# Token pieces of 384, 384, 320 and a regrouped merge in a hybrid encoder layer

## Chip, cores and metric

One core of one Trainium2 chip runs one launch of the kernel. The metric is the device time of a launch in microseconds.

## The reference

One layer of a streaming encoder for T = 1088 tokens (1024 of a new stream, 64 of a continued one) at a width of 1024, in fp32. P = RMSNorm(x) @ w_in gives the inputs of four branches of width 512, their gate paths and four merge gates of 1024 columns each. Cut to what the change touches:

```python
u = jnp.stack([u_a, u_b, u_c, u_d], axis=2)          # four branches, (B, T, 4, 512)
y_br = jnp.einsum('btnc,ncd->btnd', u, p['w_down'])  # each (512 -> 1024)
gates = jax.nn.sigmoid(merge.reshape(bsz, t, N_BRANCH, D_MODEL))
mixed = jnp.sum(gates * y_br, axis=2)
out = rms_norm(mixed @ p['w_out'], p['norm_post'])   # y = x + out
```

A is a gated linear recurrence, B a chunked state-space scan (SSD), C a convolution with a LayerNorm, D stick-breaking attention.

## The kernel before

**Operands.** Activations lie transposed: channels on the 128 partitions, tokens along the free axis. Each fp32 operand is split into a high and a low fp32r part (ScalarE copies, VectorE subtracts), and a product is three matmuls, high by high, high by low, low by high (`mm3`, L104 to L107). `hh` and `hl` hold the normed input, `w_hi` and `w_lo` 128 output columns of a weight.

**Pieces.** The tokens are cut into three pieces, `SPL` = 256, 384, 448, and `hh`, `hl` are three tiles each, one per piece. `project` (L172) makes one piece of one 128-column chunk of P: 8 steps of the contraction by 3 matmuls, 24. `proj` (L176) loads a chunk's weights and does the three pieces. The pieces are also the steps in which matrix work is fed between the steps of other chains (`Feed`, L142): `feed.step(n)` issues n pieces. In the head, pieces 0, 1, 2 of two v chunks follow the transposes of the token tiles that they need (L340 to L346).

**Order.** PE runs in the order written in the program (L188). The other engines' instructions are ordered ahead of time by a planner, from costs of its own and priorities, and run in that order; `high_priority` raises an instruction by some number of places (`W_PRIO` = 300 for weight splits). All DMAs are issued by SP, in one queue.

**Stages**, by the profile: head to 57 us, projections and attention to 585, the recurrence to 742, LayerNorm to 895 and the SSD scan to 1238, both with the merge fed in between, then the gates of the last branch to 1335, its down projection to 1383, the output to the end.

**Merge** (L674). For each of three branches, `merge` walks over eight blocks d of 128 output columns. In a step it makes a gate piece (24 matmuls, a sigmoid on ScalarE), then the down piece of the same tokens (`down`, L668: 12 matmuls), and VectorE multiplies the two out of PSUM and adds them to `mt[d]` (L696, or L698 and L699). PSUM has three buffers `pj` for both kinds. Gate weights and down weights come from the same two buffers `w_hi`, `w_lo`; one load of 512 KB holds the down weights of two blocks.

**Last branch** (L947 to L983). All its gates are made first, into `sga`. Then for each d come three down pieces, evacuated by VectorE (L967, L968), copied and split into `mh` and `ml` (L969, L974), while the output weights are split into `wo` and `wp` (L982, L983). `mh` and the first half of the output weights lie in the buffers of `hh` and `hl`. The down weights are loaded for two blocks at a time, into the other of the two buffers (L971).

**SSD scan** (L810). Each of nine chunks of 128 tokens loads `xb` (two buffers), and has four parts with feed steps of 2, 1 and 2 between them; L871 and L878 belong to `second`, L838 and L845 to `first` of the next chunk, and L881 is the last reader of `xb`.

Of the kernel before, what the change touches and what calls it, by code (L numbers as in the profile page):

```python
# [18 lines left out]
SPL = ((0, 256), (256, 384), (640, 448))  # L19
NM = 448  # L20
WHERE = [(j, i * 128 - t0) for i in range(9) for j, (t0, n) in enumerate(SPL) if t0 <= i * 128 < t0 + n]
# [5 lines left out]
LNA, LNB = (2, 2, 2), 5  # L27
# [18 lines left out]
def encoder_step(ctx, tc, x, prm, win, wdt, wdn, wout, lwa, lwx, ckT, cv_, ssd0, npre, npost, dtb, alog, dskip,  # L46
# [62 lines left out]
    def rstd(st, r, n, w=1):  # L109
        """Second quarter of st = (first quarter / n + eps) ** -0.5, with one Newton step after the table's root."""  # L110
        a, y, v, t = (st[:r, j * w:j * w + w] for j in range(4))
        V.tensor_scalar(v, a, 1.0 / n, EPS, op0=OP.mult, op1=OP.add)
        S.activation(t, v, AF.Sqrt)
        V.reciprocal(y, t)
        V.tensor_tensor(t, y, y, op=OP.mult)
        V.tensor_tensor(t, t, v, op=OP.mult)
        V.tensor_scalar(t, t, -0.5, 1.5, op0=OP.mult, op1=OP.add)
        V.tensor_tensor(y, y, t, op=OP.mult)

    class Work:  # L120
        """A chain of matrix work: its first stretch fetches operands, each later one is a piece of the tokens."""
# [20 lines left out]
    class Feed:  # L142
        """Matrix work issued between the steps of another chain."""
# [28 lines left out]
    def project(p, n, i, hi, lo):  # L172
        for k in range(8):
            mm3(p[:, :n], hi[:, k, :], lo[:, k, :], hh[i][:, k, :], hl[i][:, k, :], k == 0, k == 7)

    def proj(chunk, evac, pt=pj, done=None):  # L176
        hi, lo = weights(win[chunk])
        yield
        for i, (t0, n) in enumerate(SPL):
# [12 lines left out]
    def head(hd, g_bc, tiles):  # L192
        w = len(tiles)
        st = hd.tile([128, 4 * w], FT, name="st", bufs=4)
        xs = []
        for e, i in enumerate(tiles):
            r = 128 if i < 8 else 64
            xt = hd.tile([128, D], FT, name="xt", bufs=9)
            dma(xt[:r], x[i * 128:i * 128 + r, :])
            if i == 0:  # L200
                dma(g_bc, ap(npre, 0, [[0, 128], [1, D]]))
            if r < 128:
                V.memset(st[r:, e:e + 1], 1.0)
            sq = hd.tile([128, D], FT, name="sq", bufs=1)
            S.activation(sq[:r], xt[:r], AF.Square, accum_out=st[:r, e:e + 1])
            xs.append(xt)
        rstd(st, 128, D, w)
        for e, i in enumerate(tiles):
            r = 128 if i < 8 else 64
            hn = hd.tile([128, D], FT, name="hn", bufs=4)  # L210
            V.scalar_tensor_tensor(hn[:r], xs[e][:r], st[:r, w + e:w + e + 1], g_bc[:r], op0=OP.mult, op1=OP.mult)
            j, o = WHERE[i]
            nk = 8 if i % 2 else 4
            for q in range(0, 8, nk):
                p = pz() if nk == 8 else pg()
# [63 lines left out]
    # convolution module  # L279
# [29 lines left out]
    def spill(chunk, dst):  # L309
        def evac(t0, n, p):  # L310
            g = cp.tile([128, NM], FT, name="t3", bufs=3)
# [6 lines left out]
    def v_chunk(c, lag=2):  # L318
        def evac(t0, n, p):
            vT = cp.tile([128, NM], FT, name="t3", bufs=3)  # L320
            S.activation(vT[:, :n], p[:, :n], AF.Copy)
            dma(vT_o[c][:, t0:t0 + n], vT[:, :n])

            def turn():
                pt = pg()
                j0, nb = t0 // 128, n // 128
                for j in range(0, n, 128):
                    r = min(128, n - j)
                    PE.transpose(pt[:r, j:j + 128], vT[:, j:j + r], ident)
                S.activation(v_tok[:, j0:j0 + nb, c * 128:(c + 1) * 128],  # L330
                             pt[:, :nb * 128].rearrange("p (j c) -> p j c", c=128), AF.Copy)
                if n % 128:
                    S.activation(v_tok[:64, 8, c * 128:(c + 1) * 128], pt[:64, nb * 128:nb * 128 + 128], AF.Copy)
            feed.defer(lag, turn)
        yield from proj(C_V + c, evac)

    s0 = Work(both(v_chunk(0, 1), v_chunk(1, 1)))
# [31 lines left out]
    def k_chunk(c):  # L369
        def evac(t0, n, p):  # L370
            kt = cp.tile([128, NM], FT, name="t3", bufs=3)
# [178 lines left out]
    # RG-LRU, inputs of the SSD  # L550
# [99 lines left out]
    # merge of the branches  # L650
    ut = ctx.enter_context(tc.tile_pool(name="ut", bufs=1, reuse_waits="tile"))
    tp_ = ctx.enter_context(tc.tile_pool(name="tp", bufs=3, reuse_waits="tile"))
    mp = ctx.enter_context(tc.tile_pool(name="mp", bufs=1, reuse_waits="tile"))
    mt = [mp.tile([128, T], FT, name=f"m{d}") for d in range(8)]
# [13 lines left out]
    def down(wh, wl, e, us, i, n):  # L668
        p = pj()
        for k in range(4):  # L670
            mm3(p[:, :n], wh[:, 4 * e + k, :], wl[:, 4 * e + k, :], us[i][0][:, k, :], us[i][1][:, k, :], k == 0, k == 3)
        return p

    def merge(bi):  # L674
# [3 lines left out]
        nwd = weights(wdn[b, 0])  # L678
        yield
        for d in range(8):  # L680
            hi, lo = nxt
            if d % 2 == 0:
                wh, wl = nwd

            def gate(i, n):
                p = pj()
                project(p, n, i, hi, lo)
                sg = tp_.tile([128, NM], FT, name="sg")
                S.activation(sg[:, :n], p[:, :n], AF.Sigmoid)  # L689
                return sg  # L690

            def mix(i, t0, n, sg):
                p = down(wh, wl, d % 2, us, i, n)
                m = mt[d][:, t0:t0 + n]
# [5 lines left out]
            sgs = [gate(i, n) for i, (_, n) in enumerate(SPL)] if d + bi == 0 else None  # L700
            for i, (t0, n) in enumerate(SPL):
                mix(i, t0, n, sgs[i] if sgs else gate(i, n))
                if i == 0 and d < 7:
                    nxt = weights(win[C_MG + 8 * b + d + 1])
                    if d % 2:
                        nwd = weights(wdn[b, (d + 1) // 2])
# [4 lines left out]
    # LayerNorm of the convolution module  # L711
# [3 lines left out]
    with tc.tile_pool(name="ln", bufs=1, side="right", reuse_waits="tile") as ln:  # L715
# [16 lines left out]
        for i, (t0, n) in enumerate(SPL):  # L732
            p = pg()
            for k in range(8):
                for q, hx in enumerate((hh, hl)):
                    PE.matmul(p[:16, :n], wd2[:, k, :], hx[i][:, k, :], start=k == 0 and q == 0, stop=k == 7 and q == 1)  # L736
            S.activation(dtr[:, t0:t0 + n], p[:16, :n], AF.Copy)
        feed.step()
# [14 lines left out]
        for i, (t0, n) in enumerate(SPL):  # L753
# [13 lines left out]
            feed.step(2)  # L767
# [15 lines left out]
            feed.step(2)  # L783
# [18 lines left out]
    # SSD scan  # L802
# [7 lines left out]
    class Chunk:  # L810
# [3 lines left out]
        def first(self):  # L814
# [6 lines left out]
            xb = self.xb = sp_.tile([128, 8, 128], FT, name="xb")  # L821
# [107 lines left out]
    for i in range(9):  # L929
# [4 lines left out]
        feed.step(2)  # L934
        if prev:
            prev.fourth()
        feed.step()
        ch.second()
        feed.step(2)
        prev = ch  # L940
    prev.third()
    feed.step()
# [5 lines left out]
    us = [load_u(b, i) for i in range(3)]  # L948
    sgp = ctx.enter_context(tc.tile_pool(name="sgp", bufs=1, side="right", reuse_waits="tile"))
# [4 lines left out]
    mh = [hp.tile([128, 8, n], FR, name=f"mh{i}", tag=f"hh{i}") for i, (_, n) in enumerate(SPL)]  # L954
    wo = [[], []]
    for i, (_, n) in enumerate(SPL):
        wt_ = hp.tile([128, n // 128, 1024], FR, name=f"wo{i}", tag=f"hl{i}")
        wo[0] += [wt_[:, k, :] for k in range(n // 128)]
    ml = []
    nwd = weights(wdn[b, 0])  # L960
    for d in range(8):
        if d % 2 == 0:
            wh, wl = nwd
        g = sga[d]
        for i, (t0, n) in enumerate(SPL):
            p = down(wh, wl, d % 2, us, i, n)
            V.tensor_tensor(g[:, t0:t0 + n], p[:, :n], g[:, t0:t0 + n], op=OP.mult)  # L967
            V.tensor_tensor(g[:, t0:t0 + n], mt[d][:, t0:t0 + n], g[:, t0:t0 + n], op=OP.add)  # L968
            S.activation(mh[i][:, d, :], g[:, t0:t0 + n], AF.Copy)  # L969
        if d in (0, 2, 4):  # L970
            nwd = weights(wdn[b, d // 2 + 1])  # L971
        l_ = mp.tile([128, T], FR, name=f"ml{d}", tag=f"m{d}")
        for i, (t0, n) in enumerate(SPL):
            V.tensor_sub(l_[:, t0:t0 + n], g[:, t0:t0 + n], mh[i][:, d, :].bitcast(FT))  # L974
# [11 lines left out]
    for i in range(9):  # L986
        r = 128 if i < 8 else 64
        j, o = WHERE[i]
        xr = ut.tile([128, D], FT, name="xr", tag=f"uh{i % 2}")
        dma(xr[:r], x[i * 128:i * 128 + r, :])  # L990
        st = tp_.tile([128, 4], FT, name="ost", bufs=2)
        sq = ut.tile([128, 512], FT, name="osq", tag="uh2")
        yo = ut.tile([128, D], FT, name="yo", tag=f"ul{i % 2}")
        for e in range(2):
            p = pj() if e == 0 else pg()
            for k in range(8):
                w = wo[e][k]
                mm3(p[:r], mh[j][:, k, o:o + r], ml[k][:, i * 128:i * 128 + r], w[:, 0:512], w[:, 512:1024],
# [73 lines left out]
```

## Time and profile before

| | us |
|---|---|
| median of 3 runs | 1493.87 |
| lowest, highest | 1492.25, 1494.49 |
| profiled execution, span from first to last instruction | 1490.9 |
| PE busy | 1460.1 |
| VectorE busy | 921.1 |
| ScalarE busy | 588.5 |

The page gives the profiled execution's span; its time as a launch is not listed beside it, so the median stands for it, 3.0 us above the span. PE is the matmul engine, PEld its weight loads, DVE is VectorE, ACT ScalarE, SP the engine that issues DMAs. L106 is line 106 of the kernel before.

### The profile page before, as it was taken

How to read it: one execution, taken by the hardware profiler on the slowest of the kernel's cores; microseconds unless marked ns; L12 is line 12 of the kernel's file. 1: busy time of each engine (PE TensorE's matmuls, PEld its weight loads, DVE VectorE, ACT ScalarE, POOL GpSimd, SP SyncE). 2: the span in 40 equal slices, each digit the busy share in tenths (PEclk: the TensorE clock that was granted, in tenths of full speed). 3: DMA queues.
4: the chain of work that ended last, by engine and by line, in shares of the span. 5: the costliest groups of instructions: out<-in, count | busy, mean ns of one | idle time of the engine just before them, and what ended most of it. 6: DMA issues, size and time to landing. Idle time of an engine off the chain costs nothing.

```text
span 1490.9 us, 23008 instructions
## 1 busy us (share of the span) xinstructions
PE 1460.1 (98%) x9157; PEld 1360.5 (91%) x9157; DVE 921.1 (62%) x1379; ACT 588.5 (39%) x1000; POOL 118.9 (8%) x157
## 2 busy tenths in 40 slices
PE   6999999999999999999999999999999999999997
PEld 5898999999999998999999999999999999999885
DVE  6289589579769955677765554656655541019433
ACT  6323434443453344666644322333332332124211
POOL 0003212231221222000000000000000000000000
PEclk9999999999999999999999999999999999999999
DMA  6232212313212323454433354222621234113322
GB/s 209 75 87 63 72 61 68 103 44 89 92 46 87 98 87 109 138 117 107 116 124 116 110 169 142 82 68 83 196 78 57 75 88 148 51 43 113 99 85 71
DMA packets 103339, 144.17 MB, mean 97 GB/s; under 512 B 20800, under 2 KB 82112, under 8 KB 103232
## 3 DMA queue, kind: packets, MB, share of 16 engines
q1 hardware_dynamic: 103232, 142.71, 31.9%
q8 instruction: 72, 1.18, 0.3%
q14 instruction: 35, 0.29, 0.1%
HBM read 97.95 MB, written 40.53 MB: 93 GB/s over the span
## 4 chain that ended last, share of the span: by engine, by line
PE 87%; issue 6%; DVE 4%; DMA 1%; ACT 1%; POOL 1%; SPq 0%; DVEq 0%; POOLq 0%; ACTq 0%
PE pj L105 24%; PE pj L106 24%; PE pj L107 24%; PE pg L468 2%; PE pg L450 2%; PE pg L106 1%; PE pg L107 1%; PE pg L105 1%; DVE cvo L239 1%; PE pz L417 1%; PE pz L418 1%; PE pg L878 1%; PE pg L736 1%; PE pg L871 1%; DMA g_bc<-in_npre_dram 0%
## 5 line engine op out<-in xcount | busy, mean ns | idle before, releaser
L105 PE MATMUL pj<-hh,w_hi 128*128 128x384 f32 (+2 forms) x1920 | 637.6, 332 | 1.7 <-ACT hh L220 1.7
L106 PE MATMUL pj<-hl,w_hi 128*128 128x384 f32 (+2 forms) x1920 | 631.8, 329 | 1.8 <-DVE hl L221 1.8
L107 PE MATMUL pj<-hh,w_lo 128*128 128x384 f32 (+2 forms) x1920 | 631.5, 329 | 0.0
L105 PEld LDWEIGHTS pj<-hh,w_hi 128*128 128x128 f32 x1920 | 363.6, 189 | 16.6 <-issue 2.1
L106 PEld LDWEIGHTS pj<-hl,w_hi 128*128 128x128 f32 x1920 | 363.7, 189 | 14.4 <-DVE hl L221 2.6
L107 PEld LDWEIGHTS pj<-hh,w_lo 128*128 128x128 f32 x1920 | 363.5, 189 | 11.0
L98 DVE TENSOR_TENSOR w_lo<-w_raw,w_hi 128x1024 fp32r<-128x1024 f32 x96 | 117.5, 1224 | 226.9 <-ACT w_hi L97 226.7
L97 ACT ACTIVATE w_hi<-w_raw 128x1024 fp32r<-128x1024 f32 x96 | 101.7, 1060 | 281.7 <-PE pj L106 262.6
L239 DVE SCALAR_TENSOR_TENSOR cvo<-cbuf,p_t,cvo 128x1118 f32<-128x1118 f32 x120 | 165.6, 1380 | 2.1
L105 PE MATMUL pj<-uh,w_hi 128*128 128x384 f32 (+2 forms) x384 | 126.2, 329 | 0.0
L107 PE MATMUL pj<-uh,w_lo 128*128 128x384 f32 (+2 forms) x384 | 126.2, 329 | 0.0
L106 PE MATMUL pj<-ul,w_hi 128*128 128x384 f32 (+2 forms) x384 | 126.1, 328 | 0.0
L438 DVE TENSOR_TENSOR_SCAN fb<-fb,ones 128x128 f32<-128x128 f32 (+8 forms) x68 | 90.0, 1324 | 38.0 <-POOL fb L435 37.4
L435 POOL TENSOR_SCALAR_AFFINE_SELECT beta<-beta 128x128 f32<-128x128 f32 (+1 forms) x72 | 78.2, 1086 | 14.4 <-ACT beta L431 13.7
L698 DVE TENSOR_TENSOR sg<-pj,sg 128x256 f32<-128x256 f32 (+2 forms) x48 | 25.7, 535 | 84.9 <-PE pj L107 80.6
L689 ACT ACTIVATE sg<-pj 128x256 f32<-128x256 f32 (+2 forms) x72 | 33.7, 468 | 112.2 <-PE pj L107 112.0
L105 PEld LDWEIGHTS pj<-uh,w_hi 128*128 128x128 f32 x384 | 72.7, 189 | 2.3
L106 PEld LDWEIGHTS pj<-ul,w_hi 128*128 128x128 f32 x384 | 72.6, 189 | 2.2
L107 PEld LDWEIGHTS pj<-uh,w_lo 128*128 128x128 f32 x384 | 72.6, 189 | 2.2
L435 POOL TENSOR_SCALAR_AFFINE_SELECT fb<-fb 128x128 f32<-128x128 f32 (+1 forms) x72 | 38.2, 530 | 449.2 <-ACT fb L430 354.4
L439 DVE TENSOR_TENSOR beta<-beta,fb 128x128 f32<-128x128 f32 (+8 forms) x68 | 50.3, 740 | 4.3 <-POOL beta L435 0.7
L452 ACT ACTIVATE wT<-pg 128x512 f32<-128x512 f32 (+3 forms) x96 | 43.3, 485 | 18.1 <-PE pg L450 17.8
(313 smaller groups left out, 1683.0 us busy)
## 6 DMA issues: line engine op xcount, KB each, us to landing
w_raw<-in_win_dram SPq DMA_DIRECT2D x80, 512.0 KB, 3.7
w_raw<-in_wdn_dram SPq DMA_DIRECT2D x16, 512.0 KB, 3.6
xt<-in_x_dram SPq DMA_DIRECT2D x8, 512.0 KB, 10.5
xbc<-xs SPq DMA_DIRECT2D x8, 512.0 KB, 2.6
xb<-xbc SPq DMA_DIRECT2D x8, 512.0 KB, 4.9
w_raw<-in_wout_dram SPq DMA_DIRECT2D x8, 512.0 KB, 3.7
xr<-in_x_dram SPq DMA_DIRECT2D x8, 512.0 KB, 3.8
out_y_dram<-yo SPq DMA_DIRECT2D x16, 256.0 KB, 2.3
```

The costliest lines, as they stand in the source:

```text
L97: S.activation(hi, r3, AF.Copy)
L98: V.tensor_sub(lo, r3, hi.bitcast(FT))
L105: PE.matmul(out, ah, bh, start=first, stop=False)
L106: PE.matmul(out, ah, bl, start=False, stop=False)
L107: PE.matmul(out, al, bh, start=False, stop=last)
L239: V.scalar_tensor_tensor(out[:, :n], b[:, i:i + n], w[:, i:i + 1], out[:, :n], op0=OP.mult, op1=OP.add)
L435: G.affine_select(t_[s, 1024 - w:1024], t_[s, 1024 - w:1024], pattern=[[-1, w]], compare_op=OP.is_gt, fill=fill, base=0, channel_multiplier=1)
L438: V.tensor_tensor_scan(F[:, rev], F[:, rev], ones[:, 0:1].to_broadcast([128, n]), 1.0, OP.mult, OP.mult)
L439: V.tensor_tensor(B[:, L:1024], B[:, L:1024], F[:, L + 1:1025], op=OP.mult)
L450: PE.transpose(p[:, (j - j0) * 128:(j - j0 + 1) * 128], B[:, L + j * 128:L + (j + 1) * 128], ident)
L452: S.activation(wT[:, j0:j1, :], p[:, :(j1 - j0) * 128].rearrange("p (j c) -> p j c", c=128), AF.Copy)
L689: S.activation(sg[:, :n], p[:, :n], AF.Sigmoid)
```

## The change

The pieces become 384, 384, 320 everywhere except in the two v chunks of the head, which keep the old ones (`SPL0`). `hh`, `hl`, `mh` and the first half of the output weights become one tile each, sliced by token. In the merge a step is now one gate piece or one down piece: three gates of a block, then its three downs; all counts of feed steps in the LayerNorm and the scan are doubled. Down weights are loaded for one block (256 KB) into a pool of their own with one buffer for the raw weights, the high and the low part; the next block's are asked for behind the third down piece. The last branch uses the same function. `xb` has one buffer instead of two. The pool of the gates' tiles is closed before the last branch.

```diff
-SPL = ((0, 256), (256, 384), (640, 448))
+SPL = ((0, 384), (384, 384), (768, 320))
+SPL0 = ((0, 256), (256, 384), (640, 448))
-LNA, LNB = (2, 2, 2), 5
+LNA, LNB = (4, 4, 4), 10
...
-    hh = [hp.tile([128, 8, n], FR, name=f"hh{i}") for i, (_, n) in enumerate(SPL)]
-    hl = [hp.tile([128, 8, n], FR, name=f"hl{i}") for i, (_, n) in enumerate(SPL)]
+    hh = hp.tile([128, 8, T], FR, name="hh")
+    hl = hp.tile([128, 8, T], FR, name="hl")
...
-    s0 = Work(both(v_chunk(0, 1), v_chunk(1, 1)))
+    s0 = Work(both(v_chunk(0, 1, SPL0), v_chunk(1, 1, SPL0)))
...
+    dw = ctx.enter_context(tc.tile_pool(name="dw", bufs=1, reuse_waits="tile"))
...
+    def down_weights(b, d):
+        raw = dw.tile([128, 4, 128], FT, name="d_raw")
+        dma(raw, wdn[b, d // 2, :, d % 2 * 512:d % 2 * 512 + 512].rearrange("p (k c) -> p k c", k=4))
+        hi, lo = (dw.tile([128, 4, 128], FR, name=f"d_{f}") for f in ("hi", "lo"))
+        with tc.high_priority(offset=W_PRIO):
+            split(hi, lo, raw)
+        return hi, lo
...
-        nwd = weights(wdn[b, 0])
+        nwd = down_weights(b, 0)
         yield
         for d in range(8):
             hi, lo = nxt
-            if d % 2 == 0:
-                wh, wl = nwd
...
+            wh, wl = nwd
+            sgs = []
+            for i, (t0, n) in enumerate(SPL):
                 p = pj()
-                project(p, n, i, hi, lo)
+                project(p, t0, n, hi, lo)
                 sg = tp_.tile([128, NM], FT, name="sg")
                 S.activation(sg[:, :n], p[:, :n], AF.Sigmoid)
+                sgs.append(sg)
+                if i == 0 and d < 7:
+                    nxt = weights(win[C_MG + 8 * b + d + 1])
+                yield
+            for i, (t0, n) in enumerate(SPL):
+                p = down(wh, wl, us, i, n)
...
+                if i == 2 and d < 7:
+                    nwd = down_weights(b, d + 1)
...
-            xb = self.xb = sp_.tile([128, 8, 128], FT, name="xb")
+            xb = self.xb = sp_.tile([128, 8, 128], FT, name="xb", bufs=1)
...
-        feed.step(2)
+        feed.step(4)
...
-        feed.step()
+        feed.step(2)
         ch.second()
-        feed.step(2)
+        feed.step(4)
...
-    nwd = weights(wdn[b, 0])
+    nwd = down_weights(b, 0)
     for d in range(8):
-        if d % 2 == 0:
-            wh, wl = nwd
+        wh, wl = nwd
...
-        if d in (0, 2, 4):
-            nwd = weights(wdn[b, d // 2 + 1])
+        if d < 7:
+            nwd = down_weights(b, d + 1)
```

## Rows read from the trace of the kernel before

**Rows 1.** Page, head and part 1: busy us, share of span, instructions.
```profile
span 1490.9 us, 23008 instructions
...
PE 1460.1 (98%) x9157; PEld 1360.5 (91%) x9157; DVE 921.1 (62%) x1379; ACT 588.5 (39%) x1000; POOL 118.9 (8%) x157
```

**Rows 2.** Windows of three stages: length, busy us per engine (count), PEclk, DMA.
```profile
895.00:1238.00 343.00, 341.43 (x2176) 321.18 (x2175) 192.07 (x366) 120.71 (x164) 0.00 (x0) 1.00 0.33 99
1238.00:1335.00 97.00, 97.00 (x583) 93.33 (x582) 12.47 (x12) 19.27 (x33) 0.00 (x0) 1.00 0.21 68
1335.00:1386.00 51.00, 51.00 (x303) 48.68 (x302) 45.77 (x89) 23.54 (x43) 0.00 (x0) 1.00 0.40 124
```

**Rows 3.** PE's waits: engine, line, waited for, us in total, times, longest.
```profile
PE pg L218 <- DVE st L115: 10.0, 1, 10.0
...
PE pg L903 <- DVE cbm L847: 0.9, 2, 0.7
```

**Rows 4.** Timeline of PE, last gates: start us, us, instruction; piece starts.
```profile
1245.97 0.36 PE L105 MATMUL pj<-hh,w_hi 128*128 128x448 f32 x1
...
1250.93 0.28 PE L105 MATMUL pj<-hh,w_hi 128*128 128x256 f32 x1
...
1253.80 0.34 PE L105 MATMUL pj<-hh,w_hi 128*128 128x384 f32 x1
...
1257.97 0.36 PE L105 MATMUL pj<-hh,w_hi 128*128 128x448 f32 x1
```

**Rows 5.** Timeline of PE, scores of 320 columns in the attention.
```profile
401.83 0.31 PE L418 MATMUL pz<-kl,qs 128*128 128x320 f32 x1
...
402.26 0.34 PE L105 MATMUL pj<-hh,w_hi 128*128 128x384 f32 x1
```

**Rows 6.** Groups by form, PE, one line of the products: count, busy, mean.
```profile
L105 PE MATMUL pj<-hh,w_hi 128*128 128x384 f32 x640 | 216.4, 338 | 0.0
...
L105 PE MATMUL pj<-uh,w_hi 128*128 128x384 f32 x128 | 43.0, 336 | 0.0
```

**Rows 7.** Timeline of VectorE in the LayerNorm stage.
```profile
820.17 2.54 DVE L772 RECIPROCAL lnr<-lnr 128x384 f32<-128x384 f32 x1
822.74 1.76 DVE L773 TENSOR_TENSOR lnx<-lnx,lnr 128x1536 f32<-128x1536 f32 x1
```

**Rows 8.** Chain of waits, SSD scan: start us, us, what.
```profile
953.94 0.86 PE pg L871 x4
...
969.00 0.88 PE pg L845 x4
```

**Rows 9.** Timeline of all engines, SSD scan, one xb load.
```profile
957.85 1.10 DVE L881 SCALAR_TENSOR_TENSOR yz<-xb,dsk,pg 128x128 f32<-128x128 f32 x4
...
959.02 0.57 SPq L822 DMA_DIRECT2D xb<-xbc  x1
```

**Rows 10.** Instructions of L822, the xb loads: time to landing.
```profile
DMA to landing us min/median/max: 3.2/4.4/7.2
```

**Rows 11.** Timeline, end of the last gates: one weight split.
```profile
1334.47 0.37 PE L106 MATMUL pj<-hl,w_hi 128*128 128x448 f32 x1
...
1334.68 0.19 PEld L105 LDWEIGHTS pj<-uh,w_hi 128*128 128x128 f32 x1
1334.87 1.06 ACT L97 ACTIVATE w_hi<-w_raw 128x1024 fp32r<-128x1024 f32 x1 [4.26 <-PE pj L106]
...
1335.97 1.23 DVE L98 TENSOR_TENSOR w_lo<-w_raw,w_hi 128x1024 fp32r<-128x1024 f32 x1 [5.64 <-ACT w_hi L97]
```

**Rows 12.** Groups by form, last down stage: splits of 512 columns.
```profile
L982 ACT ACTIVATE wp<-w_raw 128x512 fp32r<-128x512 f32 x8 | 5.0, 626 | 2.9 <-DVE ml L974 2.9
...
L983 DVE TENSOR_TENSOR wp<-w_raw,wp 128x512 fp32r<-128x512 f32 x7 | 4.8, 681 | 0.0
```

**Rows 13.** Timeline, last down stage: a down piece's end and its evacuation.
```profile
1350.21 0.34 PE L107 MATMUL pj<-uh,w_lo 128*128 128x384 f32 x1
...
1352.33 0.55 DVE L967 TENSOR_TENSOR sga<-pj,sga 128x384 f32<-128x384 f32 x1
```

More of the change, by code (lines that the diff above doesn't have):

```diff
@@ L18 @@
 EPS = 1e-6
-SPL = ((0, 256), (256, 384), (640, 448))
-NM = 448
-WHERE = [(j, i * 128 - t0) for i in range(9) for j, (t0, n) in enumerate(SPL) if t0 <= i * 128 < t0 + n]
+SPL = ((0, 384), (384, 384), (768, 320))
+SPL0 = ((0, 256), (256, 384), (640, 448))
+NM, N0 = 384, 448
 KA, KC = 4, 31
@@ L170, in encoder_step, with project, proj @@
     feed = Feed()
-    def project(p, n, i, hi, lo):
+    def project(p, t0, n, hi, lo):
+        t = slice(t0, t0 + n)
         for k in range(8):
-            mm3(p[:, :n], hi[:, k, :], lo[:, k, :], hh[i][:, k, :], hl[i][:, k, :], k == 0, k == 7)
-    def proj(chunk, evac, pt=pj, done=None):
+            mm3(p[:, :n], hi[:, k, :], lo[:, k, :], hh[:, k, t], hl[:, k, t], k == 0, k == 7)
+    def proj(chunk, evac, pt=pj, done=None, spl=SPL):
         hi, lo = weights(win[chunk])
         yield
-        for i, (t0, n) in enumerate(SPL):
+        for i, (t0, n) in enumerate(spl):
             p = pt()
-            project(p, n, i, hi, lo)
+            project(p, t0, n, hi, lo)
             evac(t0, n, p)
@@ L310, in evac @@
         def evac(t0, n, p):
-            g = cp.tile([128, NM], FT, name="t3", bufs=3)
+            g = cp.tile([128, N0], FT, name="t3", bufs=3)
             S.activation(g[:, :n], p[:, :n], AF.Sigmoid)
@@ L315, in spill, with v_chunk @@
         yield from proj(chunk, evac)
-    def v_chunk(c, lag=2):
+    def v_chunk(c, lag=2, spl=SPL):
         def evac(t0, n, p):
-            vT = cp.tile([128, NM], FT, name="t3", bufs=3)
+            vT = cp.tile([128, N0], FT, name="t3", bufs=3)
             S.activation(vT[:, :n], p[:, :n], AF.Copy)
@@ L370, in evac @@
         def evac(t0, n, p):
-            kt = cp.tile([128, NM], FT, name="t3", bufs=3)
+            kt = cp.tile([128, N0], FT, name="t3", bufs=3)
             S.activation(kt[:, :n], p[:, :n], AF.Copy)
@@ L699, in mix @@
                     V.tensor_tensor(m, m, sg[:, :n], op=OP.add)
[L700 to L706, printed above, removed]
+                if i == 2 and d < 7:
+                    nwd = down_weights(b, d + 1)
                 if d == 7 and bi < 2:
@@ L735, in encoder_step @@
                 for q, hx in enumerate((hh, hl)):
-                    PE.matmul(p[:16, :n], wd2[:, k, :], hx[i][:, k, :], start=k == 0 and q == 0, stop=k == 7 and q == 1)
+                    PE.matmul(p[:16, :n], wd2[:, k, :], hx[:, k, t0:t0 + n], start=k == 0 and q == 0, stop=k == 7 and q == 1)
             S.activation(dtr[:, t0:t0 + n], p[:16, :n], AF.Copy)
-        feed.step()
+        feed.step(2)
         pd = pg()
@@ L948, in encoder_step @@
     us = [load_u(b, i) for i in range(3)]
+    ptp.close()
     sgp = ctx.enter_context(tc.tile_pool(name="sgp", bufs=1, side="right", reuse_waits="tile"))
```

51 lines of the change are left out of this document (22 added, 29 removed).

## The prediction, made blind

> **What bounds the kernel now.** I read the page first: PE is busy for 1460.1 of 1490.9 us, 98% [rows 1]. A busy PE is not yet a bound, so the next view is the sum by stage. In the SSD scan PE has 341.4 of 343 us, in the last gates 97.0 of 97, in the last down projections 51.0 of 51, all at a granted clock of 1.00 [rows 2]. The list of PE's waits says the same: the longest, 10.0 us, is in the head, whose two v chunks keep their old pieces, and in all of the merge there is 0.9 us [rows 3]. So there is hardly a stall to remove. A change can win only by making PE's own work shorter, and it loses whenever PE is made to wait. What PE's work costs must come from starts, not from durations: in the timeline of the last gates a matmul of 384 columns has a duration of 0.34 us but the next starts 0.17 us later, as they overlap [rows 4].
>
> **Part 1: pieces of 384, 384, 320 for 256, 384, 448.** From start to start a whole piece (24 matmuls) gives the price of one. 448 columns: 1245.97 to 1250.93, 4.96 us, 206.7 ns. 256 columns: to 1253.80, 2.87 us, 119.6 ns. 384 columns: to 1257.97, 4.17 us, 173.8 ns [rows 4]. At the granted 2.4 GHz the columns alone are 186.7, 106.7 and 160.0 ns, so one matmul costs 12.9 ns over its columns at 256, 13.8 at 384, but 20.0 at 448. The columns of a triple are 1088 before and after, so the pieces matter only because the widest one is dearer than the line through the others. One triple before: 206.7 + 119.6 + 173.8 = 500.1 ns.
> No 320-column matmul stands in a projection, but the attention's scores have them, on the same kind of operands. Three in a row take 0.43 us (401.83 to 402.26), with rounding 140 to 147 ns, though the weights change behind the last; the other seven such groups are alike [rows 5]. The line between 256 and 384 gives 146.7. I take 145, within both and nearer the row, which is the operation itself; the bounds are 143.3 (the row as read) and 146.7. After: 2 x 173.8 + 145 = 492.6 ns, 7.5 ns less per triple; 5.8 at the one bound, 9.2 at the other.
> How many triples: each of the three lines of a product has 640 matmuls of each width on hh and hl and 128 on the branch outputs, 768 in all, so 3 x 768 = 2304 triples [rows 6]. The first two v chunks keep the old pieces: 2 x 8 x 3 = 48. 2256 x 7.5 = 16.9 us less, 13.1 to 20.8 by the bounds. Nearly all of it lies where PE has no gap, so I count it whole. That hh, hl, mh and the first half of the output weights become one tile each costs nothing: PE keeps the written order, in which the head's later transposes stand behind the pieces that read the earlier tokens, and the first down block behind all gates.
> A rule speaks against this part. The Trainium skill, page "TensorE: Matmul & The Clock Gate", section "Back-to-back issue gap", gives a warm gap of N/2.4 plus a fixed 2.5 ns. By that a triple costs the same however 1088 columns are cut, and the part brings nothing. Here the surplus is 13 to 20 ns and grows with the width [rows 4], so the trace does not bear it out; it stays as a rival.
>
> **Part 2: gate and down pieces regrouped, steps doubled.** The products are the same in number. A gate piece is now 24 x 173.8 = 4.2 us, a down piece 2.1 us, and three downs follow each other. They share three PSUM buffers with the gates: the next gate reuses the buffer of the first down piece when the other two are through (12 x (173.8 + 145) = 3.8 us later). VectorE must have evacuated it by then, and it is in order: queued ahead can be the LayerNorm's 2.54 us reciprocal and 1.76 us product behind it [rows 7]. With 0.55 us of its own that is 4.9 us, so at worst some 1 us of stall in each of three LayerNorm pieces; before, the same reciprocals cost PE nothing [rows 3]. Every six small steps hold what three big ones held, so the cover for the other chains is the same on average; the least stretch of four is one gate and three downs, 3.5 + 5.9 = 9.4 us. 0 for this part, up to 3 us.
> xb loses its second buffer. A chunk's load then waits for the previous chunk's last reader on VectorE (L881, done at 958.95, 5.0 us behind the start of L871 at 953.94), is issued by SP within 0.7 us and lands in 4.4, at most 7.2 us [rows 8 to 10]: 10.1 to 12.9 us behind L871. Its first reader, L845, starts 15.1 us behind L871 today [rows 8]; 11.7 of these are the two steps between (448 and 256 columns, 36 matmuls each), 3.3 other products. With the least four small steps that is 9.4 + 3.3 = 12.7 us. Hidden, with 0.2 us as the worst case, and more only if SP, whose queue is in order, holds the load behind another wait. 0.8 us for xb and part 2 together, bounds -1 (VectorE has fewer evacuations in a row before a chunk) and +5.
>
> **Part 3: down weights in single buffers of their own.** Inside the merge the split for d + 1 starts when PE has left block d, and three gate pieces (11.8 us) follow before it is read. SP issues 32 loads of half the size for 16, and ScalarE and VectorE split them in two halves for one whole; none of the three is the bound there. Nothing; without that cover it would be the price of the last stage, below.
> In the last stage there are no gates: the down blocks follow each other, and seven times PE needs weights that cannot be written before it has finished with the old ones. Today one load serves two blocks and goes to the other of two buffers, and PE does not wait. The chain can be read at 1334.5: the last matmul that reads w_hi starts at 1334.47, ScalarE's copy at 1334.87 (0.40 later, 0.34 for a matmul of 0.31 instead of 0.37 us), ends at 1335.93, and VectorE starts at 1335.97 [rows 11]. With half a load the copy takes 0.63 and the subtraction 0.68 us (the output weights' splits have this shape) [rows 12]. Let T be when the next block would start. The last reader of d_hi starts at T - 0.29, the copy runs from T + 0.05 to 0.68, the subtraction from 0.72 to 1.40. The weight load runs a matmul ahead (0.2 us) [rows 11], so the third matmul, the first that needs d_lo, starts at T + 1.60 for T + 0.35. That is 1.25 us per block, and it can't be less: 7 x 1.25 = 8.8 us.
> More comes from engines that are in order and not free. ScalarE is busy 23.5 of 51 us there and VectorE 45.8 [rows 2]: half an instruction of 0.55 us times these shares is 0.13 and 0.25, and I add 0.1 for a weight DMA that arrives late, as it can be issued only when the old subtraction is done. 1.7 us per block, 7 x 1.7 = 11.9 us. At the upper end VectorE is behind as it is now at times: a down piece whose last matmul starts at 1350.21 and ends at 1350.55 is picked up at 1352.33, 1.8 us late, behind a weight split and an output split [rows 13]. 1.25 + 1.8 = 3.0 us, 21 us in all. PE's stall gives VectorE time to catch up, so I stay near the low end.
>
> **Sum.** -16.9 + 11.9 + 0.8 = -4.2 us. The page's execution spans 1490.9 us and the runs' median is 1493.87, so 3.0 us lie around the span, and they stay: 1493.9 - 4.2 = 1489.7.
>
> **Rivals.**
> (a) VectorE decides the last stage. Place: the seven block changes. It pays if the split of d_lo queues behind a late evacuation (0.55), a run of three subtractions of 1.4 us and a ScalarE copy of 0.5: 1.25 + 2.4 = 3.7 us each, 25.9 in all, 1493.9 - 16.9 + 25.9 + 0.8 = 1503.7. It decides from 2.3 us per block, where 7 x 2.3 eats the gain. For it: VectorE has 90% there, and lags of 1.8 us [rows 2, 13]. Against it: the split is raised in the planner's order (W_PRIO), and a waiting PE sends VectorE nothing.
> (b) The bare floor: 1.25 us per block and 320 columns at 143.3 ns. -20.8 + 8.8 = -12, 1481.9. For it: the raised order; against: an idle moment on two engines seven times.
> (c) The price is linear in the columns and the 320 pieces carry the 20 ns of 448. 153.3 ns, a triple of 500.9, no gain (+1.8 us): 1493.9 + 1.8 + 11.9 + 0.8 = 1508.4. The row of 320 columns speaks against it. The skill's rule above would give the same zero.
> (d) Cover runs out in the scan or the LayerNorm (xb, PSUM buffers), 5 us: 1493.9 - 16.9 + 11.9 + 5 = 1493.9, no change.
>
> **How the numbers follow.** Chances: forecast 0.50 (1484 to 1495 for itself), (a) 0.22, (b) 0.13, (c) 0.05, (d) 0.10. 0.2%, 3 us, is what a measurement of this kernel can tell from no change: below 1490.9 is faster, above 1496.9 slower. Of the forecast's half I give 0.31 to faster, 0.15 to same, 0.04 to slower; (b) is faster; (a) is 0.18 slower and 0.04 same; (c) slower; (d) 0.03, 0.05, 0.02. Faster 0.47, same 0.24, slower 0.29. The range 1481 to 1503 reaches from (b) nearly to (a).
>
> **What would show it.** Right: 24 matmuls of 320 columns take 3.5 us from start to start, those of 384 still 4.17; the last gates (eight chunks of three pieces) shrink from some 96 by 8 x 24 x 7.5 ns = 1.4 us; the list of PE's waits has a new row on the splits in down_weights, about 12 us over seven blocks, all after the last gates; the scan keeps under 2 us of waits. Wrong: 320 columns at 150 ns or more; waits of 3 us or more at the block changes; PE waiting for xb or for L696 and L698.

## The result and the profile after

The changed kernel takes 1506.13 us (median of 5, 1505.47 to 1507.52) where the kernel before took 1493.30 beside it on the same chip: ratio 1.0087, 95% interval 1.0075 to 1.0099. It is slower, 16 us above the prediction and 3 us above its range. The profiled execution spans 1504.1 us against 1490.9 [rows 1], so the 13 us are in the span and can be looked for there.

First, what did PE gain? The timeline of PE in the last gates, again the starts of three successive pieces (answering to [rows 4]; the columns are start, duration, instruction):

```profile
1258.22 0.34 PE L105 MATMUL pj<-hh,w_hi 128*128 128x384 f32 x1
...
1262.41 0.33 PE L105 MATMUL pj<-hh,w_hi 128*128 128x384 f32 x1
...
1266.57 0.31 PE L105 MATMUL pj<-hh,w_hi 128*128 128x320 f32 x1
...
1270.08 0.34 PE L105 MATMUL pj<-hh,w_hi 128*128 128x384 f32 x1
```

24 matmuls of 320 columns take 3.51 us, 146.3 ns each; of 384, 4.16 to 4.19. In the whole trace a triple went from about 500 to 493.8 ns: 6.2 ns less, times 2256 is 14.0 us. So the price of a piece fell as forecast, by a little less (16.9; the lower bound was 13.1). If all of it reached the end, some 27 us were lost elsewhere; a run further down shows that not all of it does. The list of PE's waits (answering to [rows 3]) names the largest losses:

```profile
PE pj L105 <- ACT d_hi L224: 9.6, 8, 5.6
PE pg L218 <- DVE st L115: 9.5, 1, 9.5
PE pg L851 <- issue: 3.5, 1, 3.5
...
PE pg L106 <- DVE xg L225: 2.2, 3, 1.0
```

The eight waits for `d_hi` are two things: one of 5.6 us, and seven of 0.57. L851 reads `xb`. The wait for `xg` was 0.2 us before.

**One long wait, at the start of the merge.** The first block of the first branch makes its three gates ahead of its three downs, in the kernel before too; there every other block takes gate and down in turn. PE, ScalarE and SP around 760 us, from their timelines (SP's rows are the issue of a DMA; in brackets the idle time before a row, and what ended it):

```profile
760.17 0.31 PE L107 MATMUL pj<-hh,w_lo 128*128 128x320 f32 x1
766.04 0.69 PE L105 MATMUL pj<-uh,d_hi 128*128 128x384 f32 x1 [5.56 <-ACT d_hi L224]
```
```profile
765.36 0.63 ACT L224 ACTIVATE d_hi<-d_raw 128x512 fp32r<-128x512 f32 x1 [5.07 <-DMA d_raw<-in_wdn_dram]
```
```profile
757.07 0.45 SPq L638 DMA_DIRECT2D ul<-al  x1
759.68 0.53 SPq L728 DMA_DIRECT2D lnx<-cv  x1
760.26 0.61 SPq L672 DMA_DIRECT2D d_raw<-in_wdn_dram  x1
```

The first down weights are issued at 760.26, when PE is through with the three gates that should have covered them. In SP's queue they stand behind the load of `lnx`, and that lies in memory of the recurrence and waits until `al` has been stored (SP's list of waits, first row below). It waited for that before, too, 2.0 us; new is what stands behind it. Before, the same down weights went to the shared weight buffers and were issued at 721.86 (second row, SP's timeline of the kernel before):

```profile
SPq L728 <- DMA ul<-al: 2.0, 1, 2.0
```
```profile
721.86 0.42 SPq L92 DMA_DIRECT2D w_raw<-in_wdn_dram  x1
```

The wait costs more than its length. The windows of 5 us from 760 (length, busy us of PE, PEld, DVE, ACT, POOL, PEclk, DMA share, GB/s) show the granted clock at its lower level, 1.2 GHz, behind it:

```profile
760.00:765.00 5.00, 0.48 (x4) 0.22 (x2) 0.64 (x1) 0.28 (x2) 0.00 (x0) 0.92 0.76 238
765.00:770.00 5.00, 3.96 (x12) 3.73 (x13) 3.63 (x8) 3.30 (x4) 0.00 (x0) 0.50 1.04 349
770.00:775.00 5.00, 5.00 (x29) 4.77 (x27) 3.52 (x14) 0.56 (x2) 0.00 (x0) 0.90 0.27 100
```

The Trainium skill, page "TensorE: Matmul & The Clock Gate", section "HAM oscillation — how this bites in real kernels", says that a wait for data can drop the clock and that the work behind it then starts cold. This trace agrees: 0.50 in the stretch behind the 5.6 us.

**xb.** SP and PE in the scan, then VectorE's last reader of the old `xb`:

```profile
1076.89 0.94 SPq L664 DMA_DIRECT2D ul<-ul  x1
1077.91 1.11 SPq L828 DMA_DIRECT2D xb<-xbc  x1
```
```profile
1083.27 1.09 PE L844 MATMUL pz<-lt,tri_gt 128*128 128x512 f32 x4
1087.86 1.47 PE L851 MATMUL pg<-Ct,xb 128*128 128x256 f32 x4 [3.50 <-issue]
```
```profile
1072.55 1.11 DVE L887 SCALAR_TENSOR_TENSOR yz<-xb,dsk,pg 128x128 f32<-128x128 f32 x4
```

The buffer is free at 1073.66, but SP first issues the last four of the six loads of the next branch (L664), from 1073.36 to 1077.83; the first of these had waited for PE to finish with the old tiles. The load of `xb` starts 4.3 us late and, behind these 2,816 KB (a piece of 384 and one of 320 tokens, high and low, 512 channels each), takes 9.9 us to land, where the slowest took 7.2 before [rows 10]. Behind PE's wait the granted clock reads 0.85 and 0.81 in the windows of 5 us from 1085 and 1090, so the scan loses more than the 3.5 us.

**The last down stage.** One of its seven block changes, on PE, ScalarE and VectorE:

```profile
1346.89 0.31 PE L106 MATMUL pj<-ul,d_hi 128*128 128x320 f32 x1
1347.04 0.31 PE L107 MATMUL pj<-uh,d_lo 128*128 128x320 f32 x1
1347.92 0.45 PE L105 MATMUL pj<-uh,d_hi 128*128 128x384 f32 x1 [0.57 <-ACT d_hi L224]
1348.20 0.33 PE L106 MATMUL pj<-ul,d_hi 128*128 128x384 f32 x1
1348.64 0.44 PE L107 MATMUL pj<-uh,d_lo 128*128 128x384 f32 x1
```
```profile
1347.24 0.62 ACT L224 ACTIVATE d_hi<-d_raw 128x512 fp32r<-128x512 f32 x1
```
```profile
1347.90 0.69 DVE L225 TENSOR_TENSOR d_lo<-d_raw,d_hi 128x512 fp32r<-128x512 f32 x1
```

The first matmul starts 0.88 us after the one before it (0.15 without a wait), the second 0.28 and the third 0.44 after that (0.17 each without). The next block's last L107 starts at 1354.19, so a block takes 7.15 us; its 36 matmuls at 173.7 and 146.4 ns are 5.93. That is 1.22 us per change, 8.5 in all.

The stages together, in us from the first PE matmul of each to that of the next, for the two kernels and four of the runs below. Unlike in the list of stages further up, "head" here reaches to the attention's first score. In some of the runs blocks of the merge move between the scan and the last gates, so these two are one row.

| stage | before | after | joined tiles | regrouped | three cures | regrouped, cured |
|---|---|---|---|---|---|---|
| head | 115.3 | 114.3 | 114.4 | 114.3 | 114.9 | 115.0 |
| attention | 469.8 | 467.6 | 470.0 | 467.6 | 467.6 | 467.6 |
| recurrence | 157.1 | 157.8 | 157.7 | 161.0 | 158.7 | 156.1 |
| LayerNorm | 156.7 | 163.5 | 163.3 | 160.1 | 159.8 | 156.9 |
| scan and last gates | 436.0 | 438.0 | 436.5 | 432.7 | 433.0 | 432.7 |
| last downs | 47.9 | 56.0 | 47.9 | 47.5 | 47.5 | 47.5 |
| output, to the end | 108.1 | 106.9 | 106.9 | 106.9 | 106.6 | 106.9 |

The output is 1.2 to 1.5 us shorter in each kernel of the table with joined tiles; why was not tried.

### The profile page after: what moved, and what is told of

It reads as the page before. It is cut to its first block, busy times and chain, and to the rows that moved or that the text cites. A ratio compares the mean times of both kernels' runs of the same rounds, so it can differ in the third digit from the quotient of the medians.

```text
span 1504.1 us, 23055 instructions
## 1 busy us (share of the span) xinstructions
PE 1458.4 (97%) x9157; PEld 1392.6 (93%) x9157; DVE 920.9 (61%) x1395; ACT 590.9 (39%) x1016; POOL 110.2 (7%) x157
## 4 chain that ended last, share of the span: by engine, by line
PE 79%; issue 9%; DVE 6%; ACT 3%; DMA 2%; POOL 1%; SPq 0%; DVEq 0%; POOLq 0%; ACTq 0%
PE pj L105 22%; PE pj L107 22%; PE pj L106 22%; PE pg L468 2%; PE pg L450 2%; PE pg L106 1%; PE pg L107 1%; PE pg L105 1%; DMA ul<-al 1%; DVE w_lo L98 1%; PE pz L417 1%; PE pz L418 1%; DVE xc L239 1%; DVE gx L626 1%; PE pg L884 1%
## 5 line engine op out<-in xcount | busy, mean ns | idle before, releaser
L106 PE MATMUL pj<-hl,w_hi 128*128 128x384 f32 (+2 forms) x1920 | 627.3, 327 | 1.8 <-DVE hl L221 1.8
L107 PE MATMUL pj<-hh,w_lo 128*128 128x384 f32 (+2 forms) x1920 | 627.2, 327 | 0.0
L106 PEld LDWEIGHTS pj<-hl,w_hi 128*128 128x128 f32 x1920 | 361.4, 188 | 4.0 <-DVE hl L221 2.6
L107 PEld LDWEIGHTS pj<-hh,w_lo 128*128 128x128 f32 x1920 | 361.4, 188 | 0.3
L98 DVE TENSOR_TENSOR w_lo<-w_raw,w_hi 128x1024 fp32r<-128x1024 f32 x80 | 97.9, 1224 | 207.3 <-ACT w_hi L97 207.1
L97 ACT ACTIVATE w_hi<-w_raw 128x1024 fp32r<-128x1024 f32 x80 | 84.7, 1059 | 152.1 <-PE pj L106 149.9
L105 PE MATMUL pj<-uh,d_hi 128*128 128x384 f32 (+1 forms) x384 | 128.8, 335 | 9.6 <-ACT d_hi L224 9.6
L107 PE MATMUL pj<-uh,d_lo 128*128 128x384 f32 (+1 forms) x384 | 127.2, 331 | 0.7
L106 PE MATMUL pj<-ul,d_hi 128*128 128x384 f32 (+1 forms) x384 | 126.2, 329 | 0.0
L105 PEld LDWEIGHTS pj<-uh,d_hi 128*128 128x128 f32 x384 | 72.9, 190 | 12.6 <-ACT d_hi L224 11.7
L698 ACT ACTIVATE sg<-pj 128x384 f32<-128x384 f32 (+1 forms) x72 | 33.8, 470 | 111.0 <-PE pj L107 108.3
L107 PEld LDWEIGHTS pj<-uh,d_lo 128*128 128x128 f32 x384 | 72.7, 189 | 3.2 <-DVE d_lo L225 3.2
L106 PEld LDWEIGHTS pj<-ul,d_hi 128*128 128x128 f32 x384 | 72.8, 190 | 0.3
L224 ACT ACTIVATE d_hi<-d_raw 128x512 fp32r<-128x512 f32 x32 | 20.1, 629 | 91.6 <-PE pj L106 45.0
```

Source lines behind the costliest of these rows:

```text
L97: S.activation(hi, r3, AF.Copy)
L98: V.tensor_sub(lo, r3, hi.bitcast(FT))
L105: PE.matmul(out, ah, bh, start=first, stop=False)
L106: PE.matmul(out, ah, bl, start=False, stop=False)
L107: PE.matmul(out, al, bh, start=False, stop=last)
```

## The experiments

Twelve kernels ran, each beside the kernel before on its chip (medians 1493.8 to 1494.3). Ratios are to that, with 95% intervals. A diff is against the kernel that its text names.

**Undoing one part each.** The last stage's down weights as before:

```diff
-    nwd = down_weights(b, 0)
+    nwd = weights(wdn[b, 0])          # in the last stage alone
...
-        if d < 7:
-            nwd = down_weights(b, d + 1)
+        if d in (0, 2, 4):
+            nwd = weights(wdn[b, d // 2 + 1])
```

> The new kernel with the last stage's down weights loaded two blocks at a time into the shared double buffers, as before; inside the merge the new single buffers stay. Theory A: the seven block changes lose their wait of 1.23 us (882 for 147 ns at the first matmul, 441 for 174 ns at the second), 8.6 us, so 1497.5 us (1496 to 1499). Rival F (with PE not held up, VectorE is late instead, as it was at 1352 us in the trace of before): only half comes back, 1502.

Measured: 1499.32 us, 1.0033 (1.0021 to 1.0046). The stage falls from 56.0 to 47.5 us, the 8.5 us read above, and its list of waits is empty. The ratio is 0.0054 lower than that of the changed kernel, 8.1 us. The time is 0.3 us above theory A's range; VectorE does not take the 8.5 us back, and rival F falls.

The down weights' pool in memory that is free early:

```diff
+    dw = ctx.enter_context(tc.tile_pool(name="dw", bufs=1, reuse_waits="tile"))
     ut = ctx.enter_context(tc.tile_pool(name="ut", bufs=1, reuse_waits="tile"))
     mp = ctx.enter_context(tc.tile_pool(name="mp", bufs=1, reuse_waits="tile"))
-    dw = ctx.enter_context(tc.tile_pool(name="dw", bufs=1, reuse_waits="tile"))
```

> The new kernel with the pool of the down weights allocated ahead of the branch tiles, in memory that the attention left long before (the pool came after 'mt' and lay on memory of the RG-LRU). Theory A (memory): the first d_raw is loaded before the RG-LRU ends, PE no longer waits 5.6 us for d_hi at 760 us, and the granted clock stays at 1.00 behind it (0.50 and 0.90 in the two stretches of 5 us from 765 us now): 6 to 8 us less, 1499 (1498 to 1500.5). Rival G (the start of the LayerNorm stage has no cover whatever comes first: joined tiles alone put 3.7 us there, behind ScalarE's sigmoids): another wait takes its place, at most 3 us less, 1503 to 1506.

Measured: 1503.28 us, 1.0060 (1.0048 to 1.0073), inside rival G's range. The first down weights are now loaded at 604.0 us and the wait of 5.6 us is gone, but the LayerNorm stage falls by 3.5 us, not by 7. VectorE's and PE's timelines in this run show the next wait in line:

```profile
766.70 0.96 DVE L733 TENSOR_TENSOR lns<-lnx 128x768 f32<-128x768 f32 x1 [7.01 <-DMA lnx<-cv]
...
770.99 0.55 DVE L707 TENSOR_TENSOR m<-pj,sg 128x384 f32<-128x384 f32 x1
```
```profile
771.60 0.44 PE L105 MATMUL pj<-hh,w_hi 128*128 128x384 f32 x1 [2.38 <-DVE m L707]
```

The down pieces wait in PSUM for L707, which stands in VectorE's order behind the fold of `lnx`; this load is late. Theory A is right about the load, rival G about the price.

The load of `xb` raised:

```diff
-            dma(xb[:, :, :L], xbc_d[:, :, t0:t0 + L])
+            with tc.high_priority(offset=W_PRIO):
+                dma(xb[:, :, :L], xbc_d[:, :, t0:t0 + L])
```

> The new kernel with the load of xb raised in the planner's order (by W_PRIO), so that SP issues it before the last four of six branch loads instead of behind them. Theory A (SP's order): the wait of 3.5 us before L851 at 1084 us goes, and some 0.7 us of slower clock behind it: 1502 (1501 to 1503.5). Rival H (the load is slow, not late: the branch loads, 4.2 MB, fill the DMA engines): the wait stays at 2 us or more, 1505.

Measured: 1502.41 us, 1.0053 (1.0040 to 1.0066). SP now issues the load at 1073.69, as soon as the buffer is free; of the read's wait 0.2 us is left, and scan and last gates fall from 438.0 to 433.0. One buffer is enough: what was wrong was its place in the queue.

```profile
1073.69 0.52 SPq L829 DMA_DIRECT2D xb<-xbc  x1
...
1075.02 0.85 SPq L664 DMA_DIRECT2D uh<-uh  x1
```

All three edits at once:

> The new kernel with three edits: the down weights' pool early, xb raised, and the last stage's down weights two blocks at a time. Theory A (the three waits are separate): 1506.1 less 7, 4 and 7 us, 1488 (1486 to 1490), under before by 5 us. Rival G (a cure at the start of the LayerNorm stage only uncovers the next wait): 1492 to 1495.

Measured: 1489.81 us, 0.9973 (0.9962 to 0.9984). The three ratios fell by 0.0054, 0.0027 and 0.0034, 0.0115 together; the sum run fell by 0.0114, 17.0 us. So the three costs add up, as theory A has it.

**Doing one part alone.** The new pieces with the old merge, steps and buffers, and the same with the old pieces, so that of the pieces only the joined tiles are left (against the kernel before). Both runs also keep where the changed kernel opens and closes the pool of the gates' tiles (behind that of `mt`, closed before the last branch); "joined tiles" stands for both below:

```diff
-SPL = ((0, 256), (256, 384), (640, 448))
+SPL = ((0, 384), (384, 384), (768, 320))     # the first of the two runs alone
...
-    hh = [hp.tile([128, 8, n], FR, name=f"hh{i}") for i, (_, n) in enumerate(SPL)]
+    hh = hp.tile([128, 8, T], FR, name="hh")  # so too hl, mh and wo0
```

> The kernel before with only the new pieces (384, 384, 320; hh, hl, mh and the first half of the output weights as one tile each); merge order, steps, weight buffers and xb as before. Theory A (the new kernel's loss comes from the new waits alone; its pieces gain what their timelines show): a triple costs 173.7 + 173.7 + 146.4 = 493.8 for 500 ns, 6.2 ns x 2256 = 14 us less than before, 1479 us (1477 to 1482). Rival B (what a piece saves is lost again where PE waits for other chains; the attention stage of the new kernel gained 2.2 us of the 4.4 that its pieces should give): 8 to 10 us less, 1484. Rival C (pieces bring nothing): 1493.

> The same as the run with the pieces alone, but with the old pieces 256, 384, 448: only the tiles are joined. Theory A: within 2 us of before (1491 to 1495), and a matmul of 448 columns still takes 206 ns from start to start: its surplus belongs to the width. Rival D (the 20 ns come from where the 448 columns lie, in a tile of their own with rows of 448): 448 falls to about 201 ns, some 2256 x 5 ns = 11 us less, 1482.

Measured: pieces alone 1500.19 us, 1.0042 (1.0029 to 1.0056); joined tiles with the old pieces 1499.15, 1.0035 (1.0022 to 1.0049). Every theory on record is wrong about the time: neither faster nor unchanged, but 6 and 5 us slower. The price of a matmul is as expected (206 ns for 448 columns in the joined tile), so rival D falls. In the joined-tile run all of the loss is in the LayerNorm stage (163.3 for 156.7). ScalarE's timeline there (`sg` are the sigmoids of the gates, `dtr` the raw step sizes of the scan), before and then with joined tiles, and PE with joined tiles:

```profile
753.21 0.38 ACT L689 ACTIVATE sg<-pj 128x256 f32<-128x256 f32 x1 [0.23 <-PE pj L107]
...
757.40 0.49 ACT L689 ACTIVATE sg<-pj 128x384 f32<-128x384 f32 x1 [0.48 <-PE pj L107]
```
```profile
762.08 1.06 ACT L97 ACTIVATE w_hi<-w_raw 128x1024 fp32r<-128x1024 f32 x1 [5.23 <-PE pj L106]
763.04 1.15 ACT L738 ACTIVATE dtr<-pg 16x256 f32<-16x256 f32 x3
764.21 1.28 ACT L690 ACT_TABLE_LOAD   x1
765.50 1.20 ACT L690 ACTIVATE sg<-pj 128x256 f32<-128x256 f32 x3
```
```profile
765.94 0.39 PE L105 MATMUL pj<-uh,w_hi 128*128 128x256 f32 x1 [3.69 <-ACT sg L690]
```

The sigmoids of the first block free the PSUM buffers for its down pieces. Before, the first two ran as soon as their gates were done; now the planner puts all three behind a weight copy that waits for the last gate, three copies of `dtr` and a table load. To take that wait away two of the first block's gate pieces got the wide PSUM buffer (against the joined tiles):

```diff
-                p = pj()
+                if d + bi == 0 and i < 2:
+                    wide = first_pz[0] = pz() if i == 0 else first_pz[0]
+                    p = wide[:, 512 * i:512 * i + 512]
+                else:
+                    p = pj()
```

> Joined tiles with the old pieces again, but the first block's first two gate pieces go to the wide PSUM buffer, so that the first down pieces need no buffer that ScalarE's sigmoids must free. Theory A (the loss of 5.4 us of the joined tiles is ScalarE's new order, which puts the sigmoids behind the end of the RG-LRU, a weight copy and three copies of dtr): the wait of 3.7 us at 762 us and the fall of the clock behind it (0.67, 0.65) go, 1494 (1492.5 to 1495.5). Rival I (other joined-tile effects, or the next late operand waits there): half of it stays, 1496.5 or more.

Measured: 1503.18 us, 1.0057 (1.0045 to 1.0070). The cure made its own wait: the second gate writes the tile whose first half the late sigmoid still has to read, and PE stood before it for 6.6 us.

```profile
761.84 0.69 PE L105 MATMUL pz<-hh,w_hi 128*128 128x384 f32 x1 [6.55 <-ACT sg L695]
```

It leaves the cause open. Another run asks for the price of that order alone: the kernel before, with separate tiles, and with two cures that have next to nothing to remove in it (their diff is further down) but turn ScalarE's order into the same one.

> The kernel before (its pieces, tiles, merge and buffers) with the two cures alone: early lnx, and two buffers each for xg, ah and al. Before has no wait for either to remove but 0.6 us in the RG-LRU. The cures change ScalarE's written order, though: the three sigmoids of the first block now stand behind the split of ah, a weight copy and three copies of dtr, as they do with the joined tiles. Theory K (that order alone is the price that the joined tiles showed): a wait of some 3.7 us of the first down piece for a sigmoid at 761 us, a slower clock behind it, 1493.9 + 5.4 - 0.6 = 1498.7 (1497 to 1500.5). Rival L (the loss belongs to the joined tiles): 1493.3, at most 1495.

Measured: 1500.52 us, 1.0043 (1.0029 to 1.0057), at the upper end of theory K's range; rival L falls. The wait is the same, and again the clock falls behind it, so the LayerNorm stage grows by 7.8 us, twice the wait. (With joined tiles it grew by 6.6, at a clock of 0.67 and 0.65 in the same windows.) So this order of ScalarE alone is enough for the price. What turned it in the joined-tile run, the tiles or the place of the pool, was not tried. PE's wait, ScalarE, and the clock in windows:

```profile
PE pj L105 <- ACT sg L689: 3.7, 1, 3.7
```
```profile
765.72 1.20 ACT L689 ACTIVATE sg<-pj 128x256 f32<-128x256 f32 x3
```
```profile
765.00:770.00 5.00, 3.85 (x21) 3.61 (x21) 1.06 (x3) 3.19 (x5) 0.00 (x0) 0.54 0.67 239
770.00:775.00 5.00, 5.00 (x17) 4.89 (x16) 1.67 (x8) 0.26 (x1) 0.00 (x0) 0.50 0.00 0
```

**Pieces and regrouping without the new buffers** (against the changed kernel; the last stage takes its down weights as in the first undo):

```diff
-        nwd = down_weights(b, 0)
+        nwd = weights(wdn[b, 0])
...
-                if i == 2 and d < 7:
-                    nwd = down_weights(b, d + 1)
+                if i == 2 and d in (1, 3, 5):
+                    nwd = weights(wdn[b, (d + 1) // 2])
...
-            xb = self.xb = sp_.tile([128, 8, 128], FT, name="xb", bufs=1)
+            xb = self.xb = sp_.tile([128, 8, 128], FT, name="xb")
```

> New pieces, and three gates then three downs per block with doubled steps; the down weights in the shared buffers, a load per two blocks, and xb with two buffers, as before. Theory A: regrouping costs nothing by itself, so the time is that of the pieces alone, within 3 us (1477 to 1484), and PE's waits in the LayerNorm stage, for xb and in the last down stage are gone. Rival E (the grouping itself costs: the PSUM buffers and the cover of the other chains are worse): 3 to 6 us above the pieces alone, 1482 to 1488.

Measured: 1489.96 us, 0.9974 (0.9963 to 0.9985): faster than before, but by 4 us and not by 14 (the profiled execution shows 0.7 of the 4). So the pieces with the regrouped merge win a little, and the single buffers turn that into a loss. Regrouping is no cost: this is 10 us better than the pieces alone. In the two profiles 5.6 us of it are in the LayerNorm stage, where the wait for the sigmoids is gone, and 4.1 in scan and last gates. With the old grouping PE also waited for the splits of weights, as this row of the run with the pieces alone has it (1.4 of the 3.9 us in scan and last gates; from start to start, ten matmuls that need `w_lo` are 3.0 us late there, and none with the new grouping):

```profile
PE pj L107 <- DVE w_lo L98: 3.9, 11, 1.9
```

What is left is a wait of 2.4 us for VectorE behind `lnx`, as in the run with the early pool, and 3.3 us of waits in the recurrence: the split of `xg` may not start until the store of the last `ah` from the same buffer is over. Behind the last of these waits the granted clock is at 0.68 (725 to 730 us) in the profiled execution, which is 1.9 us above the median.

```profile
683.45 1.12 ACT L224 ACTIVATE xg<-xl 128x1092 fp32r<-128x1092 f32 x1 [2.09 <-DMA uh<-ah]
```

Both can be cured (against the regrouped kernel):

```diff
 def ln_load(i):
+    gl = ln.tile([128, 4, NM], FT, name="lng", bufs=1)
+    if i == 0:
+        ln_first.append(ln.tile([16, T], FT, name="dtr", tag="lnq"))
     xl = ln.tile([128, 4, NM], FT, name="lnx", bufs=2)   # now not under ah, al
-    gl = ln.tile([128, 4, NM], FT, name="lng", bufs=1)
-    dma(xl[:, :, :n], cv_d[:, :, t0:t0 + n])
+    with tc.high_priority(offset=W_PRIO):
+        dma(xl[:, :, :n], cv_d[:, :, t0:t0 + n])
...
-ah = lp.tile([128, NA], FR, name="ah")
+ah = lp.tile([128, NA], FR, name="ah", bufs=2)           # also al, xg0, xg1
```

> New pieces and regrouped merge with the old weight buffers and two xb, and two cures: lnx lies in memory that the RG-LRU leaves early (not under ah and al, whose stores end at 760 us or later) and is loaded ahead of lng; xg, ah and al have two buffers each, so that the next split does not wait for the stores of ah and al. Theory A (what pieces and regrouping gained, 14 us, is lost to PE's waits at these two places: some 3 us each, and a slower clock behind the later one): 1490.0 less 6, 1484 (1482 to 1486.5). Rival J (VectorE and ScalarE are late there for other reasons): 1488 or more.

> The same with the old pieces 256, 384, 448. Theory A (where PE waits for nobody a triple of new pieces is 6.2 ns shorter): 2256 x 6.2 = 14 us above the run with the new pieces, about 1498 (1495 to 1500). Rival B (the RG-LRU, the attention and the LayerNorm take back what the pieces save, cures or not): at most 8 us above it.

> The new kernel with its three cures (down weights' pool early, xb raised, the last stage's down weights two blocks at a time) and the early lnx. Theory A (the wait of 2.4 us left at 768 us is VectorE's, held in its order behind the fold that waits for lnx): 1489.8 less 3, 1487 (1485 to 1488.5). Rival J: 1489 or more.

Measured: regrouped and cured 1484.19 us, 0.9932 (0.9919 to 0.9944), as theory A has it and the best of all. In its recurrence PE waits for nothing that the profile lists, and the LayerNorm keeps one wait of 1.3 us:

```profile
PE pj L105 <- DVE m L699: 1.3, 1, 1.3
```

The new kernel with its three cures and the early `lnx`: 1486.63, 0.9951 (0.9939 to 0.9964), also as expected. With the old pieces the cured kernel takes 1500.49, 1.0039 (1.0026 to 1.0053), 16.3 us more and 0.5 above theory A's range. That difference is not the pieces alone. The old pieces run into a new wait at the start of the LayerNorm stage, which is 7.3 us longer with it:

```profile
PE pg L745 <- ACT dtr L740: 4.6, 1, 4.6
```

The other stages of these two profiles differ by 7.5 us (attention 2.5, recurrence 0.5, scan and last gates 4.1, last downs 0.4). With all of the LayerNorm's own 288 triples at 6.2 ns, 1.8 us, which can't be told from the wait, that makes an estimate of some 9 us of the 14 that the price promises. The attention keeps 2.5 of 4.3 us (696 triples), the recurrence 0.5 of 1.8; why they keep no more was not tried.

## Why the prediction was wrong

The step that failed is the cover: inside the merge and for `xb`, the prediction held that single buffers cost nothing or 0.2 us, as other work of PE hides their loads. By stage, with its 7.5 ns on the triples of each, it forecast -2.2 us for the LayerNorm stage and -5.0 for scan and last gates; measured are +6.8 and +2.0. The attention and the recurrence were to gain 5.2 and 2.2 and came to -2.2 and +0.7. The last downs, forecast at +11.2, took +8.1: this error has the other sign and by luck hides 3 us of the others.

- **Part 1, the price.** Right in mechanism and nearly in size: 6.2 ns per triple for 7.5. "I count it whole" was wrong: by the estimate above, some 9 of 14 us reach the end where the waits are cured. Rival (c) fell: 146.3 ns for 320 columns is 13 over the 133.3 of the columns alone. The fixed 2.5 ns stand in the Trainium skill, page "TensorE: Matmul & The Clock Gate", section "Back-to-back issue gap", as the gap of an isolated matmul, which the section sets apart from a stream of weight loads and matmuls. This kernel is such a stream, and its trace does not show them.
- **Joined tiles "cost nothing".** Wrong by 5 us when done without the rest (with the gates' pool moved). PE's order is written by hand, as I argued, but ScalarE's is not, and I did not ask what else the planner would move. In the changed kernel the regrouped merge has another order there, so this is not a term of its 13 us.
- **Part 2, regrouping.** In the changed kernel PE's list has no wait for the merge's PSUM buffers, and none for the reciprocal, as forecast. But where the first wait is cured, PE stands 2.4 us for L707: the way through PSUM that I had named, with the fold of a late `lnx` ahead of it in place of the reciprocal. And beside the pieces alone regrouping is not 0 but 10 us less, as the old grouping has waits of its own there.
- **xb "hidden, with 0.2 us as the worst case".** This step failed. I had named the way, SP holding the load behind another wait, and left it out of the price. The undo gives 0.0034 of the ratio, 5 us, at the end of the range I gave to all of part 2.
- **Part 3 inside the merge, "nothing".** The step that failed most. The cover of 11.8 us is there for each block but the first of the first branch, whose load is issued behind the recurrence's stores. That is 5.6 us of wait, and the clock behind it; as the next wait takes its place, removing it gives 4 us.
- **Part 3 in the last stage.** The floor was right, the forecast 3.4 us too high: 1.22 us per change, for 1.25 and 1.7. The 0.45 us that I added for busy engines did not come: in the rows above ScalarE's copy starts 0.35 us behind the start of the last L106, and VectorE's subtraction 0.04 us behind the copy's end. Rival (a) fell.
- **Rival (d)** came nearest, with a chance of 0.10 and a price of 5 us. The places are those it named, the LayerNorm and `xb`; but in the LayerNorm the cover ran out for the down weights and not for PSUM, and the price is more than twice as high: the stages put 6.8 us into the LayerNorm alone, and 5 into `xb`. No case held it together with the loss of the last stage at a price above the gain. Of the signs of being right the price of 320 columns came true; that PE's waits for the down weights all stand behind the last gates, and that the scan keeps under 2 us of waits, did not.

## What to carry to other kernels

Where one engine is busy for 98% of the time and the others follow a planned order, an edit's price is not only in the instructions it changes but also in the orders that it redraws: compare the order of each queue before and after the edit at the start of each stage and each branch, where there may be no cover yet. A buffer of its own is not free memory: ask what lay there, what the load is queued behind, and what happens the first time, when the steady cover does not exist. An undo of each part alone, with its stage's time beside the total, finds such costs in a few runs. The best kernel here, without the new single buffers, then takes 1484.2 us, 0.7% under before; the changed kernel with all its cures takes 1486.6.

## What was not expected of the hardware

The surplus of a matmul over its columns at 2.4 GHz is 13 to 14 ns at 256, 320 and 384 columns and 20 at 448, in a joined tile as in a tile of its own. A wait of PE of 3.7 us lengthened its stage by 7.8 us in one run, as the granted clock read 0.54 and 0.50 in the next two stretches of 5 us, and by 6.6 in another, at 0.67 and 0.65. Behind 1.3 us of wait in the best kernel it stayed at 1.00, but behind two waits of 0.5 and 1.0 us in a row, in the regrouped kernel's recurrence, it read 0.68.
